# Gathered expert rows in a pipe of two slots, none in the last key step, their tiles' end in halves

## The chip, the core and the metric

One core of one Trainium2 chip runs the whole step. The metric is device time in microseconds of one execution, taken as the median of several runs. The engines are TensorE (PE in the rows; PEld is its weight load), VectorE (DVE), ScalarE (ACT), GpSimd (POOL) and SyncE (SP, which here only issues transfers). Each engine runs its own list of instructions in order and waits on semaphores of the others.

## The reference

A hybrid decoder layer over 528 prompt rows and 32 sample rows: two recurrent branches, merged, and then a channel mixer that picks experts by product keys. The change lies in the mixer alone:

```
s1, s2 = scores of the token's query against two sets of 128 keys
expert, gate = the best 16 of the sums s1[i] + s2[j], per token and head (8 heads); softmax
act = gelu(sum_d u_tab[expert, d] * x[d])            # one number per token and chosen expert
out = sum over the chosen experts of gate * act * v_tab[expert, :]
y = rmsnorm(x_residual + out)
```

There are 128 x 128 experts, each a row of 1024 numbers in u_tab and one in v_tab. A token has 8 x 16 = 128 chosen experts.

## The kernel before

The mixer works on tiles of 128 tokens, in two ways. Three prompt tiles (128, 256, 384) are computed **densely**: the experts are taken in 128 groups of 128. For each group the h step (`h_step`, L1493 to 1515) makes x times u of all its experts on TensorE, 24 products of 128x384, each operand split in a high and a low part (`thi`, cast on ScalarE at L1478; `tlo`, the rest, on VectorE at L1486). ScalarE applies gelu (`gh`, L1515). `before_v` then multiplies gh with a matrix of gates that is zero where an expert was not chosen (L1524, VectorE), splits it into `ghi` and `glo` (L484 and L485), and casts and splits the v rows too. The v step (`v_step`, L1545 to 1554; products at L1562) adds gh times v into the accumulators `eacc` of the three tiles, 18 products of 128x512.

The sample tile (32 tokens in four quarters) and prompt tile 0 are computed by **gathering** (`gathered`, L1331 to 1380): 32 + 128 = 160 slots. A slot fetches, for each of 128 partitions, one row of u and v (8 KB, together 1 MB) by an indirect DMA that POOL issues (L1342) into one of GA = 4 buffers `uv`. VectorE multiplies the u half with the token's x and sums (L1356: `w`, one number per partition, and a read of the accumulator that counts as a second instruction); ScalarE makes gelu of w and multiplies it with the gate (L1357, L1358); VectorE adds w times the v half to `acc` (L1363).

`gathered` is a generator and runs between the products. `fill.tick(rate)` adds `rate` to a debt and resumes the generator once for every whole unit; each resumption, a turn below, ends at a `yield`. An h step ticks four times and a v step three times, so an expert gives 7 ticks. Up to the v step of expert 34 only v steps run, with a rate of 0.38 (their h steps were done before). From then on each h step of expert v + 1 is followed by the v step of expert v, at G_RATE = (2 x 160 + 15 - 3 x 35 x 0.38) / (7 x 92 + 24) = 0.4418. The order in which the generator's instructions come into the engines' lists is fixed by this, before the program runs.

The last v step (`v_last`) closes one tile after another and adds the tile's `finish` (L1317 to 1330) to the same round of generators: residual plus accumulator (L1322), sum of squares (L490, ScalarE), scale and sum (L496), power (L498, POOL), product (L1328) and a store through SP. The last dense tile is closed in two halves, the others in one piece. At the end `fill.drain()` runs what is left.

A fetch into a uv buffer waits until acc has read the slot that held it before. The two raw buffers of u and the three of v are loaded by SP in the order of use.

Of the kernel before, what the change touches and what calls it, by code (L numbers as in the profile page):

```python
# [8 lines left out]
F32 = mybir.dt.float32  # L9
# [4 lines left out]
AF = mybir.ActivationFunctionType  # L14
ALU = mybir.AluOpType
# [4 lines left out]
P = 128  # L20
D = 1024
# [69 lines left out]
def body(tc, a):  # L91
    nc = tc.nc
    mm = nc.tensor.matmul
    V, PO, AC = nc.vector, nc.gpsimd, nc.scalar
# [4 lines left out]
    def pool(st, name, bufs=1, right=False, space=None):  # L99
        kw = {} if space is None else {"space": space}  # L100
        return st.enter_context(tc.tile_pool(name=name, bufs=bufs, side="right" if right else "left", reuse_waits="tile", **kw))

    def load(dst, src):
        nc.sync.dma_start(dst, src)
# [23 lines left out]
    T_ = {}  # L128
# [358 lines left out]
    def square_sum(xp, xt, rows):  # L487
        junk = xp.tile([P, D], mybir.dt.bfloat16, name="junk", tag="junk", bufs=1)
        ss = xp.tile([P, 1], F32, name="ss", tag="ss", bufs=6)
        AC.activation(junk[:rows, : xt.shape[1]], xt[:rows], AF.Square, accum_out=ss[:rows])  # L490
        return ss

    def rstd(sums, rows):
        r = EPS
        for ss in sums:
            V.tensor_scalar(ss[:rows], ss[:rows], 1.0 / D, r, ALU.mult, ALU.add)  # L496
            r = ss[:rows]
        PO.tensor_tensor(r, r, mhalf[:rows], ALU.pow)  # L498
        return r
# [811 lines left out]
    def finish_load(o, rows, x2):  # L1311
        load(o[:rows], x2)
        return o

    def finish(fp, o, rows, acc, out, n=1):

        w = D // n  # L1317
        parts = [slice(i * w, i * w + w) for i in range(n)]
        acc = acc.rearrange("p a b -> p (a b)")
        ss = []  # L1320
        for c in parts:
            V.tensor_tensor(o[:rows, c], o[:rows, c], acc[:rows, c], ALU.add)  # L1322
            ss.append(square_sum(fp, o[:, c], rows))
        yield
        rr = rstd(ss, rows)
        yield
        for c in parts:
            V.scalar_tensor_tensor(o[:rows, c], o[:rows, c], rr, T_["fwbc"][:rows, c], ALU.mult, ALU.mult)  # L1328
            load(out[:, c], o[:rows, c])


    def gathered(gp, ps_of, tiles):

        slots = [(i, k) for i, t in enumerate(tiles) for k in range(t[1][2])]
        uvs, accs = {}, {}

        def fetch(j):
            if j < len(slots):
                i, k = slots[j]
                ei = tiles[i][1][0]  # L1340
                uvs[j] = gp.tile([P, 2 * D], F32, name="uv", tag="uv", bufs=GA)
                PO.indirect_dma_start(out=uvs[j], out_offset=None, in_=a["uv"],  # L1342
                                      in_offset=bass.IndirectOffsetOnAxis(ap=ei[:, k : k + 1], axis=0))

        for x in range(GA - 1):
            fetch(x)
        yield
        for j, (i, k) in enumerate(slots):
            rows, (ei, gate, n), h2, end = tiles[i]
            if k == 0:  # L1350
                accs[i] = gp.tile([P, D], F32, name="acc", tag="acc", bufs=1)
            acc = accs[i]
            w = gp.tile([P, 1], F32, name="w", tag="w", bufs=4)
            fetch(j + GA - 1)
            uv = uvs.pop(j)
            V.scalar_tensor_tensor(out=uv[:, 0:D], in0=uv[:, 0:D], scalar=1.0, in1=h2, op0=ALU.mult, op1=ALU.mult, accum_out=w)  # L1356
            AC.activation(w, w, AF.Gelu)  # L1357
            AC.mul(w, w, gate[:, k : k + 1])  # L1358
            yield
            if k == 0:  # L1360
                AC.mul(acc, uv[:, D:], w)
            else:
                V.scalar_tensor_tensor(acc, uv[:, D:], w, acc, ALU.mult, ALU.add)  # L1363
            yield
            if k == n - 1:
                o2 = acc.rearrange("p (a b) -> p a b", a=2)
                if rows < P:
                    yield
                    yield
                    yield  # L1370
                    for b in range(2):
                        ps = ps_of()
                        mm(ps[:rows, :512], T_["sid"], acc[:, 512 * b : 512 * b + 512], start=True, stop=True)
                        yield
                        AC.copy(acc[:rows, 512 * b : 512 * b + 512], ps[:rows, :512])
                    yield
                    o2 = acc[:rows].rearrange("p (a b) -> p a b", a=2)
                yield from end(o2)


    NE = 128
    AH, AT = 36, 18
    GA = 4
# [3 lines left out]
    NL = 1  # L1387
# [12 lines left out]
    G_RATE = (2 * 160 + 15 - 3 * (AH - 1) * G_AHEAD) / (7 * (NE - AH) - 3 * G_END)  # L1400
# [43 lines left out]
    def experts(h2s, x2s, h2pair, ph, g_tiles, d_tiles, outs, s, ghp, es, sq):  # L1444
# [14 lines left out]
        def ps_h():  # L1459
            return php.tile([P, 512], F32, name="hps", tag="h")  # L1460
# [3 lines left out]
        def fetch(kind, e):  # L1464
            if e < NE and (kind, e) not in raws:
                t = (dp if kind == "u" else dv).tile([P, D], F32, name="traw", tag="traw" + kind, bufs=2 if kind == "u" else VB)
                load(t, a["uT"][e] if kind == "u" else a["uv"][e * P : (e + 1) * P, D : 2 * D])
                raws[kind, e] = t

        def prep(kind, e, late=False):  # L1470
            if e >= NE or (kind, e) in sp_:
                return
            fetch(kind, e)
            t = raws[kind, e]
            pl, nb = (dp, 2) if kind == "u" else (wtp, VS)
            x = pl.tile([P, D], F32R, name="thi", tag="thi" + kind, bufs=nb)
            y = pl.tile([P, D], F32R, name="tlo", tag="tlo" + kind, bufs=nb)
            AC.copy(x, t)  # L1478
            sp_[kind, e] = x, y
            if not late:  # L1480
                prep_lo(kind, e)

        def prep_lo(kind, e):
            if e < NE and (kind, e) in raws:
                x, y = sp_[kind, e]
                (PO if kind == "u" and e < sum(AQ) else V).tensor_tensor(y, raws.pop((kind, e)), x, ALU.subtract)  # L1486
                if kind == "v" or e + 2 not in (AH, AH + 1) or e >= AH:
                    fetch(kind, e + (2 if kind == "u" else VB))
# [3 lines left out]
        def h_step(e, rate, lo_at=0):  # L1492
            prep("u", e)  # L1493
            if e + 1 != AH:
                fetch("u", e + 1)
                prep("u", e + 1, True)
            x, y = sp_.pop(("u", e))
            ps = ps_h()
            for k in range(KT):
                ks = slice(k * P, k * P + P)  # L1500
                cs = slice(c0, c0 + nt)
                mm(ps[:, :nt], x[:, ks], hi[:, k, cs], start=(k == 0), stop=False)  # L1502
                mm(ps[:, :nt], x[:, ks], lo[:, k, cs], start=False, stop=False)  # L1503
                mm(ps[:, :nt], y[:, ks], hi[:, k, cs], start=False, stop=(k == KT - 1))  # L1504
                if k % 2:
                    (bg if e < AH else fill).tick(rate)
                if k == lo_at and e + 1 != AH:
                    prep_lo("u", e + 1)
            if e < AT:
                gh[e] = ga.tile([P, nt], F32, name="gh", tag="gh", bufs=AT)  # L1510
            elif e < AH - 3:
                gh[e] = gbf[:, (e - AT) * nt : (e - AT + 1) * nt]
            else:
                gh[e] = ghp.tile([P, nt], F32, name="gh", tag="gh", bufs=3)
            AC.activation(gh[e], ps[:, :nt], AF.Gelu)  # L1515
# [119 lines left out]
        accs = [accp.tile([P, 2, 512], F32, name=f"eacc{d}") for d in range(nd)]  # L1635
        dps.close()
        gp = pool(es, "gp", 1, True)
        fs = ExitStack()

        def end_of(t, rows):  # L1640
            return lambda acc: finish(T_["fp"], fins[t], rows, acc, outs[t])

        rows_of = {t: NS if t is None else P for t in g_tiles + d_tiles}
        fins = {}
# [17 lines left out]
        fp = T_["fp"] = pool(es, "fp")  # L1662
# [3 lines left out]
        for v in range(AH - 1, NE - NL):  # L1666
            if v == AH + 1:
                load(T_["fwbc"], a["fw"].to_broadcast([P, D]))
            if v >= AH + 2 and v % 4 == 0 and late:
                i, t = late.popleft()  # L1670
                fins[t] = finish_load(gb[:, i + 1], rows_of[t], x2s[t])
            if AH < v + 1 < NE:
                h_step(v + 1, G_RATE)
            v_of(v, G_RATE)
        for v in range(NE - NL + 1, NE):
            h_step(v, G_RATE)
        v_last(range(NE - NL, NE))
        es.close()
        st_.close()
# [1 line left out]
    outs = {None: a["o_y_s"]}  # L1681
# [101 lines left out]
```

## Time and profile before

| | us |
|---|---|
| median of 3 runs | 2190.22 |
| lowest and highest run | 2185.79, 2193.49 |
| the profiled execution | 2193.42 |
| its span, first to last instruction | 2191.5 |
| TensorE busy | 2082.0 (95%) |
| VectorE busy | 1578.0 (72%) |
| ScalarE busy | 863.1 (39%) |
| POOL busy | 755.3 (34%) |

The first half of the span holds the two branches, the router and the first h steps; the v steps begin at 1215 us and the last one ends at 2168 us. A matmul's record lasts longer than the distance to its successor, since matmuls are pipelined: 24 of a row have starts 0.17 us apart and durations of 0.34 us. So distances between starts say more than busy time. In a timeline the brackets at the end of a row give the engine's idle time ahead of the instruction and what ended it.

### The profile page before, as it was taken

The page shows a single profiled execution, that of the slowest core. Times are in us where ns is not written, and L with a number is a line of the kernel's source. Part 1 is how long each engine was busy: PE and PEld are TensorE (multiplying, and loading weights), DVE is VectorE, ACT ScalarE, POOL GpSimd, SP SyncE. Part 2 cuts the span into 40 slices and gives each one's busy share as a digit, 9 for nine tenths or more (in the row PEclk, how much of TensorE's full clock was granted, in tenths as well). Part 3 has the DMA queues.
Part 4 walks back from the last instruction along what each step waited for, and adds up shares of the span by engine and source line. Part 5 has one row for each costly group of instructions (what it writes and reads, how often), then busy time and mean ns, then how long its engine had stood idle before and what let it go on. Part 6 is the DMA issues. An engine that isn't in the chain of part 4 may idle for free. (4 is left out here: it accounts for less than half of the span.)

```text
span 2191.5 us, 34579 instructions
## 1 busy us (share of the span) xinstructions
PE 2082.0 (95%) x13085; PEld 1914.5 (87%) x13085; DVE 1578.0 (72%) x3100; ACT 863.1 (39%) x1591; POOL 755.3 (34%) x875
## 2 busy tenths in 40 slices
PE   7899999999999998999999999999999999999995
PEld 6888898888999998999899878989888888888884
DVE  6877667656436314899999678778878778887877
ACT  3323343333124324333477444343443443344343
POOL 3497610024442334664166111212222222222221
PEclk9999999999999998999999999999999999999998
DMA  4443334326653233231366999879998899989984
GB/s 146 128 127 111 117 127 147 124 97 196 209 163 108 88 137 132 93 103 61 118 236 263 335 327 324 324 285 352 344 325 309 332 339 336 331 318 335 331 299 162
DMA packets 199813, 478.90 MB, mean 219 GB/s; under 512 B 53440, under 2 KB 114752, under 8 KB 176096
## 3 DMA queue, kind: packets, MB, share of 16 engines
q1 hardware_dynamic: 169136, 278.50, 37.8%
q0 software_dynamic: 24752, 170.67, 20.9%
q10 hardware_dynamic: 5760, 27.53, 3.1%
q8 instruction: 103, 1.69, 0.3%
q14 instruction: 62, 0.51, 0.1%
HBM read 419.42 MB, written 54.46 MB: 216 GB/s over the span
## 5 line engine op out<-in xcount | busy, mean ns | idle before, releaser
L471 PE MATMUL gps<-pr,wh 128*128 128x272 f32 (+1 forms) x3328 | 583.3, 297 | 6.4 <-DVE pr L485 3.8
L471 PEld LDWEIGHTS gps<-pr,wh 128*128 128x128 f32 x3328 | 480.4, 191 | 14.9 <-DVE pr L485 4.7
L1486 DVE TENSOR_TENSOR tlo<-traw,thi 128x1024 fp32r<-128x1024 f32 x241 | 298.9, 1240 | 120.8 <-ACT thi L1478 120.2
L1342 POOL DMA_INDIRECT uv<-in_uv,ei x128 | 186.1, 1454 | 534.6 <-DVE acc L1363 527.1
L1504 PE MATMUL hps<-pr,tlo 128*128 128x384 f32 x1024 | 347.4, 339 | 14.5 <-DVE tlo L1486 13.6
L471 PE MATMUL gps<-pr,wl 128*128 128x272 f32 (+1 forms) x1664 | 352.8, 292 | 4.4 <-DVE wl L437 3.7
L1502 PE MATMUL hps<-pr,thi 128*128 128x384 f32 x1024 | 350.1, 342 | 1.6 <-ACT thi L1478 1.6
L1503 PE MATMUL hps<-pr,thi 128*128 128x384 f32 x1024 | 343.7, 336 | 0.0
L1478 ACT CAST thi<-traw 128x1024 fp32r<-128x1024 f32 x256 | 266.1, 1040 | 27.2 <-PE eacc L1562 13.6
L471 PEld LDWEIGHTS gps<-pr,wl 128*128 128x128 f32 x1664 | 266.3, 191 | 5.3 <-DVE wl L437 4.4
L1562 PE MATMUL eacc<-thi,ghi 128*128 128x512 f32 x768 | 241.7, 396 | 7.8 <-ACT ghi L484 7.0
L1562 PE MATMUL eacc<-tlo,ghi 128*128 128x512 f32 x768 | 241.6, 395 | 3.5
L1562 PE MATMUL eacc<-thi,glo 128*128 128x512 f32 x768 | 237.6, 390 | 0.0
L437 POOL TENSOR_TENSOR wl<-wraw,wh 128x1024 fp32r<-128x1024 f32 x60 | 144.0, 2400 | 246.1 <-ACT wh L436 242.1
L1363 DVE SCALAR_TENSOR_TENSOR acc<-uv,w,acc 128x1024 f32<-128x1024 f32 x158 | 202.3, 1280 | 33.8 <-ACT w L1358 33.8
L1357 ACT ACTIVATE w<-w 128x1 f32<-128x1 f32 x160 | 32.5, 203 | 478.3 <-DVE uv L1356 478.3
L1504 PEld LDWEIGHTS hps<-pr,tlo 128*128 128x128 f32 x1024 | 192.5, 188 | 20.8 <-DVE tlo L1486 19.6
L1502 PEld LDWEIGHTS hps<-pr,thi 128*128 128x128 f32 x1024 | 192.6, 188 | 10.2 <-ACT thi L1478 4.5
L1503 PEld LDWEIGHTS hps<-pr,thi 128*128 128x128 f32 x1024 | 192.7, 188 | 3.5
L1356 DVE SCALAR_TENSOR_TENSOR uv<-uv,h 128x1024 f32<-128x1024 f32 x160 | 194.7, 1217 | 0.1
L1562 PEld LDWEIGHTS eacc<-tlo,ghi 128*128 128x128 f32 x768 | 141.3, 188 | 47.1 <-DVE tlo L1486 18.7
L1562 PEld LDWEIGHTS eacc<-thi,ghi 128*128 128x128 f32 x768 | 140.7, 188 | 42.2 <-ACT ghi L484 18.3
(411 smaller groups left out, 3001.3 us busy)
## 6 DMA issues: line engine op xcount, KB each, us to landing
traw<-in_uT SPq DMA_DIRECT2D x128, 512.0 KB, 4.3
traw<-in_uv SPq DMA_DIRECT2D x128, 512.0 KB, 6.8
wraw<-in_W SPq DMA_DIRECT2D x104, 512.0 KB, 3.4
Wt<-wb ACTq DMA_DIRECT2D x24, 1024.0 KB, 4.4
wt<-Wt SPq DMA_DIRECT2D x15, 1536.0 KB, 13.2
st<-in_state_hgrn SPq DMA_DIRECT2D x8, 512.0 KB, 4.4
Wd<-W SPq DMA_DIRECT2D x8, 512.0 KB, 4.9
ATd<-AT SPq DMA_DIRECT2D x8, 512.0 KB, 3.6
```

What stands on the lines that cost most here:

```text
L437: E.tensor_tensor(wl, r3, wh, ALU.subtract)
L471: mm(ps[:, b, :w], x[:, k], y[:, k, b * w : b * w + w], start=(k == 0 and x is wh and y is hi), stop=(k == KT - 1 and x is wl))
L1342: PO.indirect_dma_start(out=uvs[j], out_offset=None, in_=a["uv"], in_offset=bass.IndirectOffsetOnAxis(ap=ei[:, k : k + 1], axis=0))
L1356: V.scalar_tensor_tensor(out=uv[:, 0:D], in0=uv[:, 0:D], scalar=1.0, in1=h2, op0=ALU.mult, op1=ALU.mult, accum_out=w)
L1357: AC.activation(w, w, AF.Gelu)
L1363: V.scalar_tensor_tensor(acc, uv[:, D:], w, acc, ALU.mult, ALU.add)
L1478: AC.copy(x, t)
L1486: (PO if kind == "u" and e < sum(AQ) else V).tensor_tensor(y, raws.pop((kind, e)), x, ALU.subtract)
L1502: mm(ps[:, :nt], x[:, ks], hi[:, k, cs], start=(k == 0), stop=False)
L1503: mm(ps[:, :nt], x[:, ks], lo[:, k, cs], start=False, stop=False)
L1504: mm(ps[:, :nt], y[:, ks], hi[:, k, cs], start=False, stop=(k == KT - 1))
L1562: mm(accs[d][:, b], l[:, ds_], r[:, b * 512 : b * 512 + 512], start=st, stop=en)
```

## The change

Three edits. In `gathered` the loop runs over x, one more than there are slots. A turn now issues the u sum of slot x; the next one issues the two ScalarE operations of slot x, then the weighted rows (acc) of slot x - 1, then the fetch of slot x + 3. Before, a slot's fetch ahead, u sum and ScalarE operations stood in one turn and its acc in the next. The number of buffers is still four. The last h step (expert 127) is called with rate 0, so no turn falls into it. `finish` is called for the two gathered tiles with n = 2: the residual sum, the squares, the product and the store are each made in two halves of 512 columns. The loop removed before `v_last` was empty (NL = 1).

```diff
@@ gathered @@
-        for j, (i, k) in enumerate(slots):
+        ws = {}
+
+        def scale_of(j):
+            i, k = slots[j]
+            AC.activation(ws[j], ws[j], AF.Gelu)
+            AC.mul(ws[j], ws[j], tiles[i][1][1][:, k : k + 1])
+
+
+        for x in range(len(slots) + 1):
+            if x < len(slots):
+                ws[x] = gp.tile([P, 1], F32, name="w", tag="w", bufs=4)
+                uv = uvs[x]
+                V.scalar_tensor_tensor(out=uv[:, 0:D], in0=uv[:, 0:D], scalar=1.0, in1=tiles[slots[x][0]][2], op0=ALU.mult, op1=ALU.mult,
+                                       accum_out=ws[x])
+                yield
+                scale_of(x)
+            j = x - 1
+            if j < 0:
+                fetch(GA - 1)
+                yield
+                continue
+            i, k = slots[j]
             rows, (ei, gate, n), h2, end = tiles[i]
             if k == 0:
                 accs[i] = gp.tile([P, D], F32, name="acc", tag="acc", bufs=1)
-            acc = accs[i]
-            w = gp.tile([P, 1], F32, name="w", tag="w", bufs=4)
-            fetch(j + GA - 1)
-            uv = uvs.pop(j)
-            V.scalar_tensor_tensor(out=uv[:, 0:D], in0=uv[:, 0:D], scalar=1.0, in1=h2, op0=ALU.mult, op1=ALU.mult, accum_out=w)
-            AC.activation(w, w, AF.Gelu)
-            AC.mul(w, w, gate[:, k : k + 1])
-            yield
+            acc, w, uv = accs[i], ws.pop(j), uvs.pop(j)
             if k == 0:
                 AC.mul(acc, uv[:, D:], w)
             else:
                 V.scalar_tensor_tensor(acc, uv[:, D:], w, acc, ALU.mult, ALU.add)
+            fetch(j + GA)
             yield
@@ experts @@
-            return lambda acc: finish(T_["fp"], fins[t], rows, acc, outs[t])
+            return lambda acc: finish(T_["fp"], fins[t], rows, acc, outs[t], 2)
-                h_step(v + 1, G_RATE)
+                h_step(v + 1, G_RATE if v + 1 < NE - 1 else 0)
             v_of(v, G_RATE)
-        for v in range(NE - NL + 1, NE):
-            h_step(v, G_RATE)
         v_last(range(NE - NL, NE))
```

VectorE in the loop of h and v steps, before; the numbers in the names tell buffers apart, so that an acc can be matched with the uv and w that it reads:

```order
L1363 SCALAR_TENSOR_TENSOR acc_15577<-uv_19790,w_19917,acc_15577 128x1024
L1486 TENSOR_TENSOR tlo_19956<-traw_19816,thi_19955 128x1024
L1356 SCALAR_TENSOR_TENSOR uv_19828,w_19974<-uv_19828,h2_9377 128x1024
L1363 SCALAR_TENSOR_TENSOR acc_15577<-uv_19828,w_19974,acc_15577 128x1024
L1524 TENSOR_TENSOR gh_19993<-gh_19993,wt_19265 128x384
L1486 TENSOR_TENSOR tlo_19997<-traw_19777,thi_19996 128x1024
L485 TENSOR_TENSOR glo_20003<-gh_19993,ghi_20002 128x384
L1356 SCALAR_TENSOR_TENSOR uv_19880,w_20018<-uv_19880,h2_9377 128x1024
```

The same place after the change:

```order
L1377 SCALAR_TENSOR_TENSOR acc_15643<-uv_19762,w_19885,acc_15643 128x1024
L1501 TENSOR_TENSOR tlo_19962<-traw_19822,thi_19961 128x1024
L1360 SCALAR_TENSOR_TENSOR uv_19850,w_19980<-uv_19850,h2_9377 128x1024
L1377 SCALAR_TENSOR_TENSOR acc_15643<-uv_19812,w_19923,acc_15643 128x1024
L1539 TENSOR_TENSOR gh_19999<-gh_19999,wt_19267 128x384
L1501 TENSOR_TENSOR tlo_20003<-traw_19783,thi_20002 128x1024
L485 TENSOR_TENSOR glo_20009<-gh_19999,ghi_20008 128x384
L1360 SCALAR_TENSOR_TENSOR uv_19909,w_20024<-uv_19909,h2_9377 128x1024
```

The kinds of operations stand in the same order; the acc right behind uv_19828 read w_19974 of that same slot, and the one behind uv_19850 now reads w_19923 of the slot before.

ScalarE at that place, before (w_19974 and w_20018 are the w of the two slots above):

```order
L1478 CAST thi_19955<-traw_19816 128x1024
L1357 ACTIVATE w_19974<-w_19974 128x1
L1358 ACTIVATE w_19974<-w_19974,gate_0_12171 128x1
L1515 ACTIVATE gh_19993<-hps_19958 128x384
L1478 CAST thi_19996<-traw_19777 128x1024
L484 CAST ghi_20002<-gh_19993 128x384
L1357 ACTIVATE w_20018<-w_20018 128x1
L1358 ACTIVATE w_20018<-w_20018,gate_0_12171 128x1
L1478 CAST thi_20030<-traw_19893 128x1024
```

And after the change (the same two slots have w_19980 and w_20024):

```order
L1493 CAST thi_19961<-traw_19822 128x1024
L1352 ACTIVATE w_19980<-w_19980 128x1
L1353 ACTIVATE w_19980<-w_19980,gate_0_12171 128x1
L1530 ACTIVATE gh_19999<-hps_19964 128x384
L1493 CAST thi_20002<-traw_19783 128x1024
L484 CAST ghi_20008<-gh_19999 128x384
L1493 CAST thi_20032<-traw_19895 128x1024
L1352 ACTIVATE w_20024<-w_20024 128x1
L1353 ACTIVATE w_20024<-w_20024,gate_0_12171 128x1
```

The first pair of w stood between the thi of one expert's u rows and the gh of the next h step, and still does, but its uv was issued a turn earlier; the second pair stood ahead of a thi and now stands behind it.

VectorE at the end, from the u sum that follows the second tile's product, before:

```order
L1356 SCALAR_TENSOR_TENSOR uv,w<-uv,h_9377 128x1024
L496 TENSOR_SCALAR ss<-ss 128x1
L1322 TENSOR_TENSOR gb<-gb,eacc_13580 128x512 x2
L1363 SCALAR_TENSOR_TENSOR acc<-uv,w,acc 128x1024
L1328 SCALAR_TENSOR_TENSOR gb<-gb,ss 128x1024
L496 TENSOR_SCALAR ss<-ss 128x1 x2
L1322 TENSOR_TENSOR gb<-gb,acc 128x1024
L1328 SCALAR_TENSOR_TENSOR gb<-gb,ss 128x512 x2
L496 TENSOR_SCALAR ss<-ss 128x1
L1328 SCALAR_TENSOR_TENSOR gb<-gb,ss 128x1024
```

And after the change:

```order
L1360 SCALAR_TENSOR_TENSOR uv,w<-uv,h_9377 128x1024
L496 TENSOR_SCALAR ss<-ss 128x1
L1322 TENSOR_TENSOR gb<-gb,eacc_13580 128x512 x2
L1377 SCALAR_TENSOR_TENSOR acc<-uv,w,acc 128x1024
L1328 SCALAR_TENSOR_TENSOR gb<-gb,ss 128x1024
L496 TENSOR_SCALAR ss<-ss 128x1 x2
L1360 SCALAR_TENSOR_TENSOR uv,w<-uv,h_9377 128x1024
L1328 SCALAR_TENSOR_TENSOR gb<-gb,ss 128x512 x2
L1377 SCALAR_TENSOR_TENSOR acc<-uv,w,acc 128x1024 x2
L1322 TENSOR_TENSOR gb<-gb,acc 128x512 x2
L496 TENSOR_SCALAR ss<-ss 128x1 x2
L1328 SCALAR_TENSOR_TENSOR gb<-gb,ss 128x512 x2
```

Behind the closing of the dense tiles stand one more uv and, with the one that it belongs to, two acc in a row; the gathered tile's sum, its two scale operations and its product are in halves at the very end.

## Rows read from the trace of the kernel before

**Rows 1.** Stretches of the expert stage: busy us (instructions) of each engine, clock, DMA.
```profile
core 0: us, PE busy (x) PEld busy (x) DVE busy (x) ACT busy (x) POOL busy (x), PEclk, DMA share, GB/s
1215.00:1387.00 172.00, 170.12 (x755) 139.26 (x756) 136.78 (x184) 72.37 (x131) 29.87 (x26) 1.00 0.92 332
1387.00:1535.00 148.00, 147.75 (x740) 131.61 (x739) 112.39 (x140) 60.82 (x119) 35.63 (x24) 1.00 0.87 317
1535.00:2152.00 617.00, 603.09 (x2963) 526.22 (x2962) 494.02 (x610) 246.56 (x501) 158.03 (x109) 1.00 0.89 325
2152.00:2169.00 17.00, 13.78 (x63) 10.85 (x62) 15.01 (x19) 5.31 (x13) 2.69 (x2) 1.00 0.52 185
```

**Rows 2.** Timeline of TensorE: start, duration, instruction; first products of h and v steps.
```profile
1387.38 0.34 PE L1502 MATMUL hps<-pr,thi 128*128 128x384 f32 x1
...
1438.38 0.34 PE L1502 MATMUL hps<-pr,thi 128*128 128x384 f32 x1
...
1449.01 0.34 PE L1502 MATMUL hps<-pr,thi 128*128 128x384 f32 x1
...
2064.91 0.34 PE L1502 MATMUL hps<-pr,thi 128*128 128x384 f32 x1
...
2069.08 0.63 PE L1562 MATMUL eacc<-thi,ghi 128*128 128x512 f32 x2
...
2073.19 0.34 PE L1502 MATMUL hps<-pr,thi 128*128 128x384 f32 x1
...
2082.58 0.34 PE L1502 MATMUL hps<-pr,thi 128*128 128x384 f32 x1
...
2152.51 0.34 PE L1502 MATMUL hps<-pr,thi 128*128 128x384 f32 x1
...
2157.40 0.63 PE L1562 MATMUL eacc<-thi,ghi 128*128 128x512 f32 x2
...
2163.81 0.73 PE L1562 MATMUL eacc<-thi,ghi 128*128 128x512 f32 x2 [2.14 <-ACT ghi L484]
```

**Rows 3.** Timeline of VectorE and ScalarE in the loop, brackets: idle time ahead.
```profile
2061.84 1.28 DVE L1363 SCALAR_TENSOR_TENSOR acc<-uv,w,acc 128x1024 f32<-128x1024 f32 x1 [0.60 <-ACT w L1358]
...
2069.28 1.22 DVE L1356 SCALAR_TENSOR_TENSOR uv<-uv,h 128x1024 f32<-128x1024 f32 x1
...
2070.54 0.20 ACT L1357 ACTIVATE w<-w 128x1 f32<-128x1 f32 x1 [2.23 <-DVE uv L1356]
...
2070.97 1.03 ACT L1478 CAST thi<-traw 128x1024 fp32r<-128x1024 f32 x1
...
2072.04 1.23 DVE L1486 TENSOR_TENSOR tlo<-traw,thi 128x1024 fp32r<-128x1024 f32 x1 [1.54 <-ACT thi L1478]
```

**Rows 4.** Waits of VectorE from 1535 to 2152: us in total, times, longest.
```profile
DVE tlo L1486 <- ACT thi L1478: 63.6, 67, 1.5
DVE gh L1524 <- ACT gh L1515: 34.1, 35, 1.0
DVE acc L1363 <- ACT w L1358: 24.5, 41, 0.6
```

**Rows 5.** Tile uv, landing of its gathers; GB/s in 40 slices from 1215 to 2165.
```profile
DMA to landing us min/median/max: 5.4/8.1/14.2
...
GB/s 386 310 306 353 323 285 354 316 344 309 236 361 345 318 377 315 303 359 331 287 375 312 304 385 301 299 372 312 315 368 311 315 360 307 302 379 308 294 303 217
```

**Rows 6.** Timeline of VectorE at the end; stores: KB each, us to landing.
```profile
2167.76 1.21 DVE L1322 TENSOR_TENSOR gb<-gb,eacc 128x1024 f32<-128x1024 f32 x1
...
2181.07 1.41 DVE L1328 SCALAR_TENSOR_TENSOR gb<-gb,ss 128x512 f32<-128x512 f32 x2 [0.44 <-POOL ss L498]
...
2183.21 1.28 DVE L1328 SCALAR_TENSOR_TENSOR gb<-gb,ss 128x1024 f32<-128x1024 f32 x1 [0.66 <-POOL ss L498]
...
out_o_y_p<-gb SPq DMA_DIRECT2D x3, 512.0 KB, 2.6
...
out_o_y_p<-gb SPq DMA_DIRECT2D x2, 256.0 KB, 2.0
```

## The prediction

> **What bounds the kernel now.** I read the stretches first. From 1215 us to 2169 us the expert products run, and TensorE counts as busy 97 to 99% there, VectorE 80%, the DMA engines some 90%, at a granted clock of 1.00 [rows 1]. Busy time hides small losses of a pipelined engine, so I went on to the starts of its steps. One expert is one h step (24 products of 384 columns) and one v step (18 of 512). Undisturbed it takes 2073.19 - 2064.91 = 8.28 us, of which the h step has 4.17 and the v step 4.11; the next expert takes 2082.58 - 2073.19 = 9.39 us [rows 2]. From the first of the regular h steps (expert 39, at 1387.38) to the last (expert 127, at 2152.51) there are 88 intervals in 765.13 us, 8.695 us each, where 88 x 8.28 = 728.6 would do [rows 2]. **36.5 us** are lost there. One interval, 1438.38 to 1449.01, holds the two extra products of the sample tile and is 2.35 us longer for them [rows 2]; they stay. So 34.1 us can go at most.
>
> Whose loss is it? TensorE is idle for 0.25 of the 148 us from 1387 to 1535, and for 13.9 of the next 617 [rows 1]: first it lives on work prepared ahead, then it is paced by whoever prepares. The preparers are VectorE and ScalarE, which wait for each other in their own order. Around 2069 us the reader sees it: VectorE does uv (L1356); ScalarE, idle for 2.23 us until then, does the two tiny w operations and only then the cast thi, which stands behind them in its queue; VectorE meanwhile waits 1.54 us for that thi to make tlo [rows 3]. Eight us earlier acc (L1363) waits 0.60 us for the w of the uv just ahead of it [rows 3]. From 1535 to 2152 the first sort makes up most of the 63.6 us in 67 waits of tlo for thi: in the timeline they come in two sizes, 33 of about 1.54 (50.8 us) and 34 of 0.38 (12.9 us), which add up to that row. The second is 24.5 us in 41 waits [rows 4]. Both are waits of VectorE for a w that was asked for just before: 75.3 us over 617/8.695 = 71 experts, 1.06 us each, and VectorE's lag behind TensorE is 0.42 (8.695 - 8.28).
>
> **The change, part by part.**
> *The pipe of two.* The count of operations in the loop does not change. On VectorE the order has the same shape; only acc now belongs to the slot before. On ScalarE the w pair goes in one turn later than its uv, behind at least one more VectorE operation, and the thi that stood behind it does not wait for a fresh uv. So the 41 waits of 0.60 go, since w was made two turns earlier, and the waits of 1.54 go, since their chain (uv, w, w, thi, tlo) is cut at its first link. What VectorE then needs per expert is its busy time, 494.0/71 = 6.96 us [rows 1], and what is left of its waits, (34.1 + 12.9)/71 = 0.66 us [rows 4]: 7.62 us, under TensorE's 8.28. TensorE then sets the pace. How much of its own idle stays I bound by the nearest stretches [rows 1]: 0.17% idle from 1387 to 1535, next to nothing; 1.1% from 1215 to 1387, half of the 2.25% of the long stretch, so 17 us would stay. The first has the same h steps, v steps and slots as the loop, the second has v steps alone; I take a value near the first, 4 us. **Loop: -30 us** (bounds -34.1 and -17).
>
> *The longer hold of a buffer.* A slot's uv buffer is now held from uv to acc over three turns, not one, so the gather into it starts later. The rate gives 7 x 0.4418 = 3.09 turns per expert, two per slot; four buffers come round in eight turns. Before, a gather has 7 turns less the 1.28 us of acc: 7 x 8.695/3.09 - 1.28 = 18.4 us. After, 5 turns: 5 x 8.28/3.09 - 1.28 = 12.1 us. Landing takes 8.1 us in the median, 14.2 at worst [rows 5]. So the median gather still arrives 4 us ahead, the worst does not, and VectorE has 0.66 us of spare per expert (8.28 - 7.62) to take that up. I cost it at 0 and keep it as a rival. The cover is thin: it was 10 us. The gathers' queue moves past nothing else, since POOL does little but gathers there.
>
> *The load of the transfers.* The same bytes in less time: 325 GB/s from 1535 to 2152 [rows 1] times 8.695/8.28 is 341. Slices of 24 us carry 385 and 386 GB/s [rows 5], so the rate is there. The Trainium skill, DMA: Bandwidth & Descriptors, section Specifications, puts the memory's limit per core at about 358 GB/s, and in its section Bandwidth lets a core streaming alone do better; no run here has a second core. By that limit 341 would be 95% of all there is and gathers would queue longer; by the slices at 386 the limit does not hold here, and the sum stays as it is either way.
>
> *No slots in the last key step.* Before, the last h step is stretched, 2157.40 - 2152.51 = 4.89 against 4.17, and the last v products wait 2.14 us for ghi, since uv, acc, uv, acc stood ahead of gh and tlo on VectorE [rows 2, 6]. After, one uv and one acc stand there. The h step gains 0.7 us. The first end sum (L1322 on the first accumulator) starts 2167.76 - 2157.40 = 10.36 us after the h step's end before [rows 2, 6]; after, it comes behind the v step of 126 (4.11), a third of that of 127 (1.37), a little start-up: 5.9 us, so 4.5 sooner. But one uv (1.22) and two acc (2 x 1.28) more stand behind it [rows 3], and the gathered tile's end now has two sums that depend on each other (an estimate: 0.2 us). The list of rows from there to the end of the last product, 2183.21 + 1.28 - 2167.76 = 16.7 us before [rows 6], grows by 4.0. **4.0 - 4.5 - 0.7 = -1.2 us.**
>
> *The end in halves.* The last product takes 1.41 us in two halves for 1.28 in one [rows 6], is counted above, and the last store is 256 KB, 2.0 us, for 512 KB, 2.6 us [rows 6]: **-0.6 us**. For the sample tile it is hidden in the loop.
>
> *From 1215 to 1387* I take 0; the most it could give is the 1.9 us of idle [rows 1].
>
> Sum: -30 - 1.2 - 0.6 = -31.8. The profiled execution took 2193.42, so 2161.6; the median of the runs is 3.2 lower, so 2158.4, **2159 us**.
>
> **The rivals.**
> *Part only.* The w pair is gone from the way, but thi and ghi still stand behind gh, and gh behind TensorE (34.1 us of waits [rows 4] are of that kind). For it speaks the stretch of 1.1% idle, against it the 148 us without any. Then 17 us stay: 2190.2 - 17 - 1.8 = 2171, and with late gathers now and then 2178.
> *No change.* VectorE's order has the same shape, tlo still stands behind uv and acc, and if that order, not the waits, paced the loop, nothing would move. Against: 6.96 us busy in 8.695. 2188 to 2190.
> *Slower: the gather paces the loop.* With hold and landing L, eight turns are L + 1.28 + 3 turns, so an expert takes (L + 1.28) x 3.09/5 us. That is 8.28 at L = 12.1 and 8.695 at L = 12.8: from a mean landing of 12.8 us on the change loses. At 13.0 it is 8.825, 88 x 0.13 = 11.4 us: 2190.2 + 11.4 - 1.8 = 2200. For it: the worst landing of 14.2 and a load that rises by 5%. Against: the median of 8.1, and that the load falls again once VectorE waits. By the 358 GB/s of the Trainium skill this would be likelier than I hold it.
>
> **How the numbers follow.** Forecast (TensorE paces the loop) 0.72, part only 0.14, no change 0.07, gathers late 0.07. The low end takes all 34.1, the 1.8 and the 1.9 of the early stage, 2152.4, and a little over 1 us for the spread of medians: 2151. The high end lies past "part only" at 2180. About 0.3% (6.6 us) is what a measurement of this kernel can tell from no change. Faster by more: 0.86; within: 0.07; slower: 0.07.
>
> **What would show it.** Right: intervals of h steps of 8.28 nearly throughout; no wait of acc for w; waits of tlo for thi only of the 0.4 kind; gathers landing at 8 to 9 us. Wrong: uv waiting for its gather more than a few times, or waits of tlo for thi of 1 us and more at other places. The end is right if the first end sum starts some 6 us behind the last h step, and wrong if TensorE still waits 2 us for ghi there.

## The result, and the profile after

| us | before | after |
|---|---|---|
| median (lowest to highest), 4 runs each | 2190.85 (2185.79 to 2193.49) | 2157.92 (2156.32 to 2158.31) |
| the profiled execution, its span | 2193.42, 2191.5 | 2158.23, 2156.5 |
| start of expert 39's h step | 1387.38 | 1386.39 |
| 88 intervals, to the start of expert 127's h step | 765.13 | 731.84 |
| from there to the end of the last product on VectorE | 31.98 | 31.38 |
| from there to the end of the span | 7.0 | 6.9 |

The ratio on record is 0.9842, with a 95% interval of [0.9826, 0.9857]; the quotient of the two medians is 0.985. The kernel is faster by 33 us, far outside the 0.3% that a measurement can tell. The forecast was 2159. The last four rows of the table split the 35.0 us between the two spans: 1.0 before the loop, **33.3 in the loop**, 0.6 and 0.1 behind it. The rows of the kernel after that they are read from, on TensorE and VectorE (before: [rows 2, 6]):

```profile
1386.39 0.34 PE L1517 MATMUL hps<-pr,thi 128*128 128x384 f32 x1
...
2118.23 0.34 PE L1517 MATMUL hps<-pr,thi 128*128 128x384 f32 x1
...
2128.07 1.22 DVE L1322 TENSOR_TENSOR gb<-gb,eacc 128x1024 f32<-128x1024 f32 x1
...
2148.19 1.42 DVE L1328 SCALAR_TENSOR_TENSOR gb<-gb,ss 128x512 f32<-128x512 f32 x2 [0.73 <-POOL ss L498]
```

The stretches after the change, with the columns of [rows 1] (the loop now ends at 2118, so the third ends at 2115):

```profile
1215.00:1387.00 172.00, 169.88 (x760) 141.02 (x761) 139.60 (x189) 72.90 (x133) 29.47 (x26) 1.00 0.93 334
1387.00:1535.00 148.00, 147.41 (x743) 132.33 (x742) 113.46 (x144) 62.56 (x122) 33.40 (x24) 1.00 0.86 317
1535.00:2115.00 580.00, 580.00 (x2943) 529.08 (x2942) 491.69 (x608) 246.18 (x500) 144.02 (x110) 1.00 0.92 345
```

In the long stretch TensorE has no idle time at all; before it had 13.9 us. The transfers run faster, 345 GB/s for 325. The whole page says the same in its chain of work that ended last. Before:

```profile
DVE 13%; PE 10%; issue 5%; ACT 5%; DMA 1%; POOL 0%; DVEq 0%; POOLq 0%
```

And after:

```profile
PE 65%; DVE 6%; DMA 4%; issue 3%; ACT 2%; POOL 1%; SPq 0%; ACTq 0%; DVEq 0%; POOLq 0%
```

The chain has moved from VectorE and ScalarE onto TensorE. The waits of VectorE from 1535 to 2115, to be held against [rows 4] (total us, times, longest):

```profile
DVE gh L1539 <- ACT gh L1530: 50.7, 57, 1.0
DVE tlo L1501 <- ACT thi L1493: 32.4, 79, 3.1
DVE uv L1360 <- DMA uv<-in_uv,ei: 4.9, 6, 1.3
```

The wait of acc for w is gone. Of tlo for thi there are more waits than before, but 77 of the 79 take 0.4 us or less; the other two, of 1.6 and 3.1 us, stand behind a thi that waited for a load of u. The waits of gh have grown from 34.1 to 50.7 us, since VectorE is now ahead of TensorE and waits for its next h step; that costs nothing while TensorE has no idle time. ScalarE and VectorE in the loop after the change (start, duration, instruction, idle time ahead), where [rows 3] shows them before:

```profile
2057.69 0.52 ACT L484 CAST ghi<-gh 128x384 fp32r<-128x384 f32 x1
2057.83 1.23 DVE L1501 TENSOR_TENSOR tlo<-traw,thi 128x1024 fp32r<-128x1024 f32 x1 [0.38 <-ACT thi L1493]
2058.11 0.20 ACT L1352 ACTIVATE w<-w 128x1 f32<-128x1 f32 x1
2058.34 0.30 ACT L1353 ACTIVATE w<-w,gate 128x1 f32<-128x1 f32 x1
2058.54 1.04 ACT L1493 CAST thi<-traw 128x1024 fp32r<-128x1024 f32 x1
2058.97 0.55 DVE L485 TENSOR_TENSOR glo<-gh,ghi 128x384 fp32r<-128x384 f32 x1
2059.44 1.28 DVE L1377 SCALAR_TENSOR_TENSOR acc<-uv,w,acc 128x1024 f32<-128x1024 f32 x1
2060.63 1.22 DVE L1501 TENSOR_TENSOR tlo<-traw,thi 128x1024 fp32r<-128x1024 f32 x1
```

The two w operations start behind ghi with no idle time, since their uv was done long ago. The thi behind them is finished at 2059.58, and the tlo that reads it starts at 2060.63 right behind acc. Before, a w of [rows 3] waited 2.23 us for its uv and a tlo 1.54 us for the thi behind that w.

The expert products still do not run quite without a gap. Of the 88 intervals, 86 are 8.28 us; one, with the sample tile's products, is longer by 2.35 as before, and one is 9.14. That last one goes back to a late load. SP, ScalarE and TensorE there:

```profile
1475.86 0.57 SPq L104 DMA_DIRECT2D wt<-Wt  x1
...
1478.62 12.93 SPq L104 DMA_DIRECT2D traw<-in_uv  x1
...
1491.65 0.37 SPq L104 DMA_DIRECT2D traw<-in_uT  x1
...
1503.38 1.05 ACT L1493 CAST thi<-traw 128x1024 fp32r<-128x1024 f32 x1 [8.57 <-DMA traw<-in_uT]
...
1505.75 0.44 PE L1519 MATMUL hps<-pr,tlo 128*128 128x384 f32 x1 [0.59 <-DVE tlo L1501]
```

An issue on SP took 12.93 us, the loads behind it in the queue came late, a thi waited 8.57 us, and of that 0.59 us reached TensorE. The last section returns to it.

### The profile page after: what moved, and what is told of

The parts are those of the page before. It is cut to its first block, busy times and chain, and to the rows that moved or that the text cites. A ratio compares the mean times of both kernels' runs of the same rounds, so it can differ in the third digit from the quotient of the medians.

```text
span 2156.5 us, 34564 instructions
## 1 busy us (share of the span) xinstructions
PE 2063.1 (96%) x13085; PEld 1925.2 (89%) x13085; DVE 1576.8 (73%) x3106; ACT 864.0 (40%) x1595; POOL 738.1 (34%) x875
## 4 chain that ended last, share of the span: by engine, by line
PE 65%; DVE 6%; DMA 4%; issue 3%; ACT 2%; POOL 1%; SPq 0%; ACTq 0%; DVEq 0%; POOLq 0%
PE eacc L1577 21%; PE gps L471 17%; PE hps L1519 7%; PE hps L1517 7%; PE hps L1518 7%; PE pw L1449 2%; DMA traw<-in_uv 1%; DVE o L1429 1%; DVE tlo L1501 1%; DMA Wt<-wb 1%; PE py L796 1%; PE py L795 1%; PE pt L1203 1%; DMA traw<-in_uT 1%; DMA uv<-in_uv,ei 0%
## 5 line engine op out<-in xcount | busy, mean ns | idle before, releaser
L1342 POOL DMA_INDIRECT uv<-in_uv,ei x128 | 170.2, 1330 | 523.0 <-DVE acc L1377 510.0
L1577 PEld LDWEIGHTS eacc<-tlo,ghi 128*128 128x128 f32 x768 | 143.9, 188 | 32.4 <-DVE tlo L1501 1.7
L1577 PEld LDWEIGHTS eacc<-thi,glo 128*128 128x128 f32 x768 | 143.9, 188 | 31.0 <-DVE glo L485 0.7
```

The costliest lines, as they stand in the source:

```text
L1577: mm(accs[d][:, b], l[:, ds_], r[:, b * 512 : b * 512 + 512], start=st, stop=en)
```

## The experiments

The theory, **A**: what paced the loop was the place of the w pair in ScalarE's queue, ahead of a cast for which VectorE waits; with that gone TensorE paces. The rivals: **B**, the pipe is needed, since acc waited for w too; **C**, the gain came from another part of the change; **D**, TensorE was the bound all along. In what follows "lost" is the time of the 88 intervals less 88 x 8.28 = 728.6 and the 2.35 of the sample tile: 34.1 us before, 0.9 after.

| kernel | lost in the loop of the profiled run, us | ratio to before |
|---|---|---|
| after | 0.9 | 0.9842 [0.9826, 0.9857] |
| before, w pair a turn later | 0.0 | 0.9848 [0.9820, 0.9876] |
| after, w pair right behind its uv | 22.5 | 0.9951 [0.9933, 0.9968] |
| after, three buffers | 49.5 | a single run, 2217.37 us |
| after, both edits at the end undone | 0.0 | 0.9851 [0.9820, 0.9881] |
| after, rate 0.456 | 0.0 | 0.9779 [0.9751, 0.9806] |
| before, w pair a turn later, rate 0.452 | 0.0 | 0.9802 [0.9772, 0.9832] |

**The w pair alone.** The kernel before, with nothing but the two ScalarE operations moved behind the `yield`, so that they open the turn of acc:

```diff
             V.scalar_tensor_tensor(out=uv[:, 0:D], in0=uv[:, 0:D], scalar=1.0, in1=h2, op0=ALU.mult, op1=ALU.mult, accum_out=w)
+            yield
             AC.activation(w, w, AF.Gelu)
             AC.mul(w, w, gate[:, k : k + 1])
-            yield
```

> The kernel before with one edit: the two ScalarE operations on w (gelu, times gate) are issued one turn later, at the head of acc's turn. acc still belongs to the same slot, a uv buffer is held one turn as before, and the last key step and the end are as before. Theory A, ScalarE's queue: what paced the loop was thi standing behind a w pair whose uv had only just been issued. Then this edit alone does it: h steps 8.28 us apart, waits of tlo for thi of the 1.5 kind gone, waits of acc for w still there (0.6 us or so, 30 to 60 of them, harmless under 8.28), 2190 - 33 = 2157 to 2160 us. Theory B, the pipe: what mattered is that acc no longer asks for a w made just before; here it still does, and even later, so 2188 us or slower and intervals of 8.7 on average.

Measured: 2159.07 us (2152.81 to 2160.27), for 2190.68 (2183.97 to 2195.75) of the kernel before, measured beside it. All intervals but that of the sample tile are 8.28. The h steps of experts 39 and 127, and stretch and waits of VectorE of this kernel, 1535 to 2115, columns as above:

```profile
1391.69 0.34 PE L1502 MATMUL hps<-pr,thi 128*128 128x384 f32 x1
...
2122.69 0.34 PE L1502 MATMUL hps<-pr,thi 128*128 128x384 f32 x1
```

```profile
1535.00:2115.00 580.00, 580.00 (x2944) 529.07 (x2943) 492.73 (x606) 246.17 (x496) 154.15 (x108) 1.00 0.93 345
```
```profile
DVE tlo L1486 <- ACT thi L1478: 28.3, 62, 4.3
DVE acc L1363 <- ACT w L1359: 24.5, 41, 0.6
```

The wait of acc for w stands there as in [rows 4], 24.5 us in 41 waits, and TensorE still has no idle time. Of the waits of tlo for thi two are above 1 us here, where before there were 33. So A holds and B falls: two lines in another order bring the whole gain, and the pipe of two is not needed for it. The end gains as well: from the start of the last h step to the end of the last product this kernel takes 28.65 us, for 31.98 before.

**The pipe without the late w.** The changed kernel, with the w pair back behind its uv; the pipe stays:

```diff
                                        accum_out=ws[x])
-                yield
                 scale_of(x)
+                yield
```

> The changed kernel with one edit undone: the w pair is issued in the same turn as its uv again; acc still belongs to the slot before, ends as changed. Theory A, ScalarE's queue: waits of tlo for thi of the 1.5 kind come back (some 30 to 50 of them), only acc's waits for w stay away. Those were 24.5/71 = 0.35 us per expert, so VectorE needs at least 8.695 - 0.35 = 8.35, more if the chain moves: intervals of 8.35 to 8.65, 6 to 32 us slower than the changed kernel, I take 2178 us. Theory B, the pipe: as the changed kernel, 2158 us, no wait of acc for w and intervals of 8.28.

Measured: 2182.5 us (2174.61 to 2184.18). Intervals of 8.28 alternate with longer ones of mostly 8.6 to 9.3, 8.535 in the mean without the sample tile's products. Waits of VectorE, 1535 to 2115:

```profile
DVE tlo L1501 <- ACT thi L1493: 70.4, 96, 1.5
```

No acc waits for a w, and the long waits of tlo for thi are back: 32 of 1.5 us, for the 33 before; the others take 0.4 or less. The chain is seen in the same kernel:

```profile
2045.01 1.22 DVE L1360 SCALAR_TENSOR_TENSOR uv<-uv,h 128x1024 f32<-128x1024 f32 x1
...
2046.28 0.20 ACT L1352 ACTIVATE w<-w 128x1 f32<-128x1 f32 x1 [3.69 <-DVE uv L1360]
2046.51 0.30 ACT L1353 ACTIVATE w<-w,gate 128x1 f32<-128x1 f32 x1
2046.71 1.04 ACT L1493 CAST thi<-traw 128x1024 fp32r<-128x1024 f32 x1
...
2047.78 1.22 DVE L1501 TENSOR_TENSOR tlo<-traw,thi 128x1024 fp32r<-128x1024 f32 x1 [1.54 <-ACT thi L1493]
```

Taking away the waits of acc alone is worth 34.1 - 22.5 = 11.6 us, taking away the long ones of tlo alone, as the experiment ahead shows, all 34.1. The two do not add up, since below 8.28 a shorter path on VectorE buys nothing.

**Fewer products on TensorE.** Both kernels without the `lo` products of all h steps (16 products for 24; this is the part left out), to see what paces each:

```diff
-                mm(ps[:, :nt], x[:, ks], lo[:, k, cs], start=False, stop=False)
```

> The kernel before without the second of the three products of each h step (high part of u times low part of x is left out in all 128 h steps, so 16 products for 24). Undisturbed, an expert then takes 8.28 - 8 x 0.173 = 6.9 us on TensorE. If VectorE and ScalarE pace the loop of the kernel before, as the prediction says, the intervals between its h steps stay at 8.6 to 8.75 us in the mean. If TensorE's own work paces it and the waits only add to it, they shrink by about the 1.4 us that is left out, to 7.3. The time as a whole falls in both cases, since the first 36 h steps get shorter too, so the intervals decide.

Before: 2177.23 us in a single run. The h steps of experts 39 and 127 in it:

```profile
1371.52 0.44 PE L1502 MATMUL hps<-pr,thi 128*128 128x384 f32 x1 [0.37 <-ACT thi L1478]
...
2136.04 0.44 PE L1502 MATMUL hps<-pr,thi 128*128 128x384 f32 x1 [0.37 <-ACT thi L1478]
```

The 88 intervals take 764.52 us, for 765.13 with all products: 8.69 us in the mean in both. A third fewer products per h step bring the loop nothing, so D falls: TensorE did not pace the kernel before.

> The changed kernel with the same third of the h products left out. By the prediction VectorE's need per expert is now 6.96 us busy and 0.66 us of waits left, so intervals of 7.0 to 7.6 us, well under the 8.7 that the kernel before should keep. If the change only hid a wait of TensorE and left the pace of the other engines as it was, 8.3 to 8.7. If the gathers cannot follow, (L + 1.28) x 3.09/5 with L of 10 us or more gives 7.0 at least, and uv waits for its gather for tens of us.

After: 2112.59 us in a single run, 7.86 us in the mean without the sample tile's extra products. That is more than A expected, 7.0 to 7.6, though well below 8.28, so TensorE did pace the changed kernel. The mean hides two things: runs of intervals of 6.93, and about every eight experts two long ones, up to 15.9 us. Stretch, and waits in it:

```profile
1535.00:2080.00 545.00, 506.35 (x2367) 437.52 (x2366) 480.97 (x602) 240.77 (x493) 140.51 (x108) 0.97 0.97 363
```
```profile
DVE tlo L1501 <- ACT thi L1493: 52.8, 47, 6.1
ACT thi L1493 <- DMA traw<-in_uT: 52.3, 11, 8.3
...
PE hps L1517 <- ACT thi L1493: 25.3, 8, 4.6
DVE uv L1360 <- DMA uv<-in_uv,ei: 10.7, 12, 1.8
```

The runs of 6.93 are about what 8.28 leaves without eight products of 0.17 us. The long intervals come from the transfers: the DMA engines are busy 97% of the time, and TensorE waits through thi for loads of u. The expectation priced late gathers, but not late loads of u.

**The hold of a buffer.** The changed kernel with `GA = 3` instead of 4:

> The changed kernel with three uv buffers for four. By the rival of the prediction (the gather paces the loop) six turns are landing L + 1.28 + 3 turns of hold, an expert takes (L + 1.28) x 3.09/3. At L = 8.1 that is 9.66 us, at L = 7 (the load falls as the loop slows) 8.53. So intervals of 8.5 to 9.7, 2180 to 2280 us, and long waits of uv for its gather, well over 100 us in all. If the hold of the buffers is not what bounds a late gather, the loop stays at 8.28 and the time at 2158.

Measured in a single run: 2217.37 us; 88 intervals in 780.52 us, without the sample tile's products 8.84 us each. Waits of VectorE, 1535 to 2100, and the landing of the gathers:

```profile
DVE uv L1360 <- DMA uv<-in_uv,ei: 112.0, 63, 5.1
```
```profile
DMA to landing us min/median/max: 5.2/7.3/10.5
```

Six turns with three of them held leave three for the fetch, so by the prediction's formula (7.3 + 1.28) x 3.09 / 3 = 8.84 us, the mean that was measured. That the two agree to the last digit is in part luck: the formula prices every interval alike, while 55 of the 88 are still at 8.28 to 8.31 and the others reach 12.6. The mechanism of the slower rival exists and its price is right in the mean of this one run; with four buffers it is not reached.

**Without the two edits at the end.** The changed kernel with the turns of the last h step and the end norm in one piece again:

```diff
-            return lambda acc: finish(T_["fp"], fins[t], rows, acc, outs[t], 2)
+            return lambda acc: finish(T_["fp"], fins[t], rows, acc, outs[t])
-                h_step(v + 1, G_RATE if v + 1 < NE - 1 else 0)
+                h_step(v + 1, G_RATE)
```

> The changed kernel with both edits of the end undone: turns fall into the last key step again, and the gathered tiles end in one piece. By the terms of the prediction the two were worth 1.2 + 0.6 us, so 2159.7 us; from the last h step's start to the end of the last product 0 to 2 us more than the changed kernel's 31.4. If the end edits are worth nothing or cost time because the one slot more at the end is not hidden, 2155 to 2158. The loop is as in the changed kernel, 8.28.

Measured: 2157.46 us (2152.49 to 2160.82); the times can't tell it from the changed kernel. The trace can: from the start of the last h step to the end of the last product it takes 28.63 us, not 31.38. The expectation had the sign wrong. VectorE at the last h step in this kernel:

```profile
2119.42 1.22 DVE L1360 SCALAR_TENSOR_TENSOR uv<-uv,h 128x1024 f32<-128x1024 f32 x1
2120.56 1.28 DVE L1377 SCALAR_TENSOR_TENSOR acc<-uv,w,acc 128x1024 f32<-128x1024 f32 x1
2122.81 0.56 DVE L1539 TENSOR_TENSOR gh<-gh,wt 128x384 f32<-128x384 f32 x1 [0.96 <-ACT gh L1530]
```

In the changed kernel:

```profile
2118.54 1.28 DVE L1377 SCALAR_TENSOR_TENSOR acc<-uv,w,acc 128x1024 f32<-128x1024 f32 x1
2123.13 0.56 DVE L1539 TENSOR_TENSOR gh<-gh,wt 128x384 f32<-128x384 f32 x1 [3.31 <-ACT gh L1530]
```

The uv and acc that the last h step no longer holds would have run while VectorE waits for TensorE anyway: it is idle for 3.31 us now, 0.96 with them. They come back at the end, where nothing covers them.

**Which of the two.** The changed kernel with the end norm in one piece, still without turns in the last h step:

```diff
-            return lambda acc: finish(T_["fp"], fins[t], rows, acc, outs[t], 2)
+            return lambda acc: finish(T_["fp"], fins[t], rows, acc, outs[t])
```

> The changed kernel with only the halves of the end norm undone: each tile's end norm is one piece with one store of 512 KB again; the last key step still takes no turns. The two edits at the end together took 31.38 us from the start of the last h step to the end of the last product, against 28.63 us with both undone. If the missing turns of the last key step are what costs: 31.0 to 31.8 us here, as in the changed kernel. If the halves are what costs: 28.3 to 29.0 us. From the last product's end to the span's end, 6.9 us in the changed kernel: by the prediction's store term 0.6 us more here, 7.5; by the trace of the changed kernel, which had gained 0.1, 7.0. The h steps stay at 8.28 us, and the time within 2154 to 2163 us.

Measured in a single run: 2159.63 us; from the last h step's start at 2119.43 to the end of the last product, 2149.42 + 1.28, 31.27 us, and 7.0 us from there to the end of the span (2157.7). The missing turns are what costs, 31.27 - 28.63 = 2.6 us. The halves are worth nothing either way: 0.1 us against them up to the last product, 0.1 for them behind it.

**More turns in the loop.** With TensorE as the bound VectorE has room in the loop, so slots can be drawn forward from the end. The changed kernel with a higher rate:

```diff
-    G_RATE = (2 * 160 + 15 - 3 * (AH - 1) * G_AHEAD) / (7 * (NE - AH) - 3 * G_END)
+    G_RATE = 0.456
```

> The changed kernel with a rate of 0.456 turns per tick in place of 0.4418, so that the last slots fall into the loop and not behind it. VectorE has 0.66 us of spare per expert and the higher rate asks for 0.1 slots more per expert at most, 0.24 us. If that spare is real, intervals stay at 8.28 and the end, from the start of the last h step to the end of the last product, falls from 31.4 to some 19 to 21 us: two slots and more of VectorE's work leave it. 2146 to 2149 us, ratio 0.980. If VectorE is at its limit, or the gathers are, the loop pays it back: 2155 or more.

Measured: 2145.55 us (2141.15 to 2150.11), ratio 0.9779 [0.9751, 0.9806], an interval wholly below that of the changed kernel. Stretch, a wait, and the last product on VectorE:

```profile
1535.00:2100.00 565.00, 565.00 (x2869) 515.57 (x2868) 485.99 (x600) 239.70 (x490) 145.48 (x109) 1.00 0.94 352
```
```profile
DVE uv L1360 <- DMA uv<-in_uv,ei: 3.2, 3, 1.6
```
```profile
2131.11 1.41 DVE L1328 SCALAR_TENSOR_TENSOR gb<-gb,ss 128x512 f32<-128x512 f32 x2 [0.73 <-POOL ss L498]
```

TensorE stays without idle time, the gathers still arrive, and the last h step starts at 2112.57, so that the end takes 2132.52 - 2112.57 = 19.95 us for 31.38. This version beats both kernels.

**The same on the short edit.** The kernel before with the w pair a turn later and a rate of 0.452:

> The kernel before with the w pair one turn later (as in the run of that edit alone), and a rate of 0.452. Ends in one piece, turns in the last key step too. If the place of the w pair is all that the loop needs, this does as well as the changed kernel with its higher rate: intervals of 8.28, the end 19 to 21 us, 2146 to 2149 us, and its gathers keep the longer lead. If acc's own waits for w (0.6 us each) come to count at the higher rate, intervals of 8.3 to 8.5 in places and 2150 to 2160 us.

Measured: 2152.52 us (2142.18 to 2158.35), ratio 0.9802 [0.9772, 0.9832]; intervals of 8.28, 19.99 us at the end. The interval reaches into that of the kernel ahead and into that of the change, so which of the two edits is the better ground for a higher rate stays open.

## Why the prediction was right, point by point

*What bounds the kernel.* VectorE, held up by its waits on ScalarE, paced the kernel before: shown, since a third fewer products per h step left its intervals at 8.69 us. The reading of 34.1 us as the most that could go was right as well: 33.3 went, and 34.1 with the w pair alone.

*The pipe of two, -30.* Measured -33.3. The mechanism was right, the term 3 us small. The step that was off is the idle time that stays on TensorE: the prediction kept 4 us by the nearest stretches, 0.9 stayed, all of it in one interval and from a load. VectorE's need of 7.62 us under TensorE's 8.28 was the right comparison; the waits that remained were even larger than the 0.66 us forecast, (50.7 + 32.4) / 70 experts = 1.19 us, but they are now slack.

One inference fell. The prediction added both kinds of wait, 75.3 us, and let the pipe remove them. Only the waits of tlo for thi had to go: with the 41 waits of acc still there the loop lost nothing. What does the work is that the w pair goes in a turn later; the pipe is one way to that, and not the shortest.

*The longer hold, 0.* Right, and narrower than it looks: over the whole run uv waited 8 times for its gather, 6.7 us together, all swallowed by VectorE's slack. So two of the signs named for being wrong showed faintly, these waits and the two of tlo above 1 us, and neither cost time. The trace of the changed kernel has no landing times of its gathers; with the same loop and the end edits undone they are 5.4/8.0/12.8 us, where the prediction had 8 to 9 in the median and decided at a mean of 12.8. With three buffers the same formula gave the mean that was measured.

*The load, 341 GB/s.* Measured 345 at a share of 0.92. The Trainium skill's memory limit per core of about 358 GB/s (DMA: Bandwidth & Descriptors, section Specifications) was not reached here. The higher rate came to 352, and the changed kernel with fewer products to 363 GB/s over 545 us, and [rows 5] has slices of up to 386; so the limit as a fixed number does not hold on this core alone. That agrees with what the Trainium skill says of a core streaming alone (DMA: Bandwidth & Descriptors, section Bandwidth).

*No slots in the last key step, -1.2.* The first end sum starts 2128.07 - 2122.40 = 5.67 us behind the end of the last h step, 5.9 were forecast, and TensorE's wait for ghi is gone: in the last two v steps the first products on each accumulator stand 1.36 to 1.39 us apart, also where the last step begins, at 2126.51:

```profile
2122.40 0.63 PE L1577 MATMUL eacc<-thi,ghi 128*128 128x512 f32 x2
...
2125.15 0.62 PE L1577 MATMUL eacc<-thi,ghi 128*128 128x512 f32 x2
2126.51 0.62 PE L1577 MATMUL eacc<-thi,ghi 128*128 128x512 f32 x2
2127.87 0.62 PE L1577 MATMUL eacc<-thi,ghi 128*128 128x512 f32 x2
```

So the signs that were named came true, and still the attribution was wrong. With the turns left in, the first end sum stands at the same distance from the last h step's start (2127.75 - 2117.91 = 9.84, and 2128.07 - 2118.23 = 9.84). The gains of 4.5 and 0.7 come from VectorE no longer lagging; the edit itself only brings the added work. The w pair alone is enough: in the kernel before with nothing else moved that distance is 10.47 us, for 15.25 before, TensorE does not wait for ghi either, and the last product ends 28.65 us behind the last h step's start. The pipe alone gives 28.63 - 31.98 = -3.3 us at the end, the missing turns +2.6, the halves +0.1, together the -0.6 that was measured. C, in so far as it is this edit, falls: it costs.

*The end in halves, -0.6.* Measured 0 by undoing it: what the shorter last store gives, 0.1 us, the two-part product takes again. The step that failed is the store term: the difference of the two landing times of [rows 6], 2.0 and 2.6 us, did not come back as time, 7.0 us behind the last product in one piece and 6.9 in halves.

*From 1215 to 1387, 0.* The start of the loop moved by 1.0 us, and all of it in this stretch, since the first v step starts at 1215.5 us in both kernels. In the kernels above whose work up to there is the same, the time from the first v step to expert 39 lies between 170.1 and 176.0 us, so nothing is read from it.

The sum was -31.8 for a measured -35.0 between the spans: a loop term 3.3 us too small, 1.1 us too much gain at the end (-1.8 for -0.7), and 1.0 us ahead of the loop that was not forecast. The errors have both signs and partly cancel. That the median still came within 1.1 us of the 2159 is in part luck: the 3.2 us by which the profiled execution of before lay above its median were taken off, and that of after lies 0.3 above its own. Of the rivals, *no change* is excluded by the intervals of 8.28, *part only* by TensorE having no idle time from 1535 to 2115. *The gather paces the loop* is a real mechanism that needs one buffer fewer.

## What to carry to other kernels

When an engine with slack does a tiny operation on a result that another engine has only just been asked for, look at what stands behind that operation in its queue: here 0.5 us of work on one number per partition, placed one turn too early, held up a cast, and the busiest preparer waited 1.5 us for it. Moving just that operation back is worth trying before a deeper pipe, which costs hold time on the buffers. And before work is taken out of a step, look whether the engine waits in it anyway; and once another engine is the bound, draw work forward from the uncovered end.

## What the runs showed of the hardware

An SP issue right behind a 1.5 MB load of gates (`wt`) can take long. In the changed kernel most issues take 0.3 to 0.6 us; the seven above 4 us between 1380 and 2100 are all loads of v, each within 6 us behind one of the ten loads of `wt`:

```profile
1541.31 0.43 SPq L104 DMA_DIRECT2D wt<-Wt  x1
1546.24 7.68 SPq L104 DMA_DIRECT2D traw<-in_uv  x1
```

Loads ordered behind such an issue can be late, as the one shown above that cost TensorE 0.59 us. In the kernel with fewer products on TensorE an issue on SP reached 13 us, and the long intervals came every eight experts, at the pace of these loads. What SP waits for inside such an issue the traces do not show, and no run here tried a split `wt` load.

The second is the rate itself. Gathers of 1 MB land in 8.1 us in the median at a DMA share of 0.89 and 325 GB/s, in 8.0 to 9.0 at 0.93 to 0.95 and 346 to 352 from 1535 to 2100 (the four kernels of the table that lose 0.0), and TensorE loses nothing; at 0.97 and 363, in the kernel with fewer products, they take 9.2, 16.1 at worst, and late loads of u cost TensorE time. Whether the higher share makes those loads late, or the slow issues on SP in a loop that asks for its loads sooner, no run here separates.
